# Latent attention in a two-layer decoder: two late weight splits and one late set of key copies placed between its first steps, and the low part of its values one step behind the rounding

## The chip, the core and the metric

The program runs on one core of one Trainium2 chip. The time is the device time of the whole program in microseconds, from one launch that computes all of the two layers. All arithmetic in question is in fp32 and in fp32r, a rounded form that TensorE takes; a number is held as a high part (rounded) and a low part (the difference), and a product is made of three matmuls: high by high, low by high, high by low.

## The reference, cut to what matters

The reference is a two-layer causal decoder on a (1, 512, 1024) input. Layer 0 runs a latent attention (8 heads) and a differential attention (4 heads) side by side, layer 1 two other attentions; each layer ends in a gated convolutional feed-forward. The part that the change touches is the latent attention of layer 0:

```python
c_q, c_kv, k_rope, dq, dk, dv = split_cols(h @ w_in, EVEN_SPLITS)
q = heads_first(rms_norm(c_q, cq_g) @ w_uq, MLA_HEADS)
q_nope, q_rope = q[..., :MLA_NOPE], rope(q[..., MLA_NOPE:], pos)
kv = heads_first(rms_norm(c_kv, ckv_g) @ w_ukv, MLA_HEADS)
k_nope, v_mla = kv[..., :MLA_NOPE], kv[..., MLA_NOPE:]
...
s = (jnp.einsum('bhqd,bhkd->bhqk', qn, k_nope)
     + jnp.einsum('bhqr,bkr->bhqk', qr, k_rope)).astype(jnp.float32) * scale
s = jnp.where(kpos[None, :] <= qpos[:, None], s, -jnp.inf)
p = jax.nn.softmax(s, axis=-1)
return jnp.einsum('bhqk,bhkd->bhqd', p.astype(v.dtype), v)
```

## The kernel before

The sequence of 512 tokens is cut into 4 tiles of 128. Activations stand transposed (features on the partitions), and every weight passes through one stream, the class `Weights`. A unit of the stream is a block of 128 x 1024. It is loaded into a raw buffer (three of them, `wraw`) on SyncE's queue, ScalarE rounds it into `wh` (L84, a CAST in the profile), and VectorE subtracts, `wl = wraw - wh` (L85). There are five pairs of `wh` and `wl`. `W.next()` hands out the next unit, having made `W.depth` units from there on; `W.ahead(n)` makes units up to number n. A raw buffer is loaded again only when VectorE has subtracted from it, so the place of a split also sets when the load of a later unit leaves SyncE's queue. The helper `mm3` (L325, L326, L327) issues the three matmuls of a product.

The latent attention lies between about 43 and 117 us of the span. It has two stages.

**Projections** (L1120 to L1157 of the program before). Six blocks `auq` make the queries: VectorE multiplies four of them by a table of the rotary angles (L1138, tiles `mq`, sixteen instructions in all), ScalarE scales the other two (L1135). Four products `auk` make the keys of two heads each, which ScalarE copies into `mk` (L1151, L1152), and four products `auv` make the values, which it copies into `mv` (L1157). The TensorE order here is written by hand; ScalarE's and VectorE's are the scheduler's.

**Steps** (L1161 to L1259). A unit of work is a pair of heads `p2` and a tile `i` of 128 queries, 16 in all, with i running fastest. A unit of tile i has i+1 tiles of keys. Its parts are:

- `score`: TensorE multiplies queries by keys into two PSUM banks of the tag `s`, one for each head (`sps`, L1166). VectorE adds the mask and finds the minimum (L1170; the profile calls it CUSTOM_DVE_ANT_0), which frees the bank. ScalarE takes the exponential with its row sum (L1173).
- `shares`: VectorE's reciprocal (L1179) and two scalings (L1181).
- `turn`: TensorE transposes the two matrices into the banks `t` and `n` (`tpp`, L1193); VectorE copies out the one (L1204), ScalarE the other (L1202).
- `value`, once for each pair of heads: TensorE multiplies the transposed shares by `mv` into the bank `o` (L1211); what it returns is the split of that bank into the high part `omh` (ScalarE, L230) and the low part `oml` (VectorE, L231).

There are only two `s` banks, so the scores of one unit need the mask step of the unit before to be done. Between the parts stand `fill`s, pieces of another projection that TensorE can do at any time: the values `av` of the differential attention, 32 pieces of three matmuls, in the order of the weight blocks. Its weights are four units of the stream, `wv[0]` to `wv[3]`, each used for two pieces of a query tile.

The list `plan` (18 rows) orders it. In row n come: `score(n)`; one entry of `left`, if there is one; some fills; `value`, if unit n-2 was the last of its heads; `turn(n-1)`; `shares(n)`; some fills. At n = 8, and at the end, one and two further units of the stream are split. TensorE, VectorE and ScalarE issue in exactly the order written there. After it comes the differential attention, whose first scores (`sps<-dqk`, L1311) the scheduler may place between the last rows of the plan.

Each engine issues its own list strictly in that order, so an instruction that waits holds all behind it on the same engine.

Of the kernel before, what the change touches and what calls it, by code (L numbers as in the profile page):

```python
# [9 lines left out]
F32 = mybir.dt.float32  # L10
# [3 lines left out]
ALU = mybir.AluOpType  # L14
# [84 lines left out]
def trunk(tc, A, out):  # L99
    nc = tc.nc  # L100
    PE, ACT, DVE, POOL = nc.tensor, nc.scalar, nc.vector, nc.gpsimd

    with ExitStack() as top:
# [15 lines left out]
        def bank(tag, name, *shape):  # L119

            t = pp.tile([P, S], F32, tag=tag, name=name, bufs=BANKS[tag])
            if not shape:
                return t[:]
            n = math.prod(shape)
            names = "abc"[:len(shape)]
            return t[:, :n].rearrange(f"p ({' '.join(names)}) -> p {' '.join(names)}",
                                      **dict(zip(names, shape)))
# [78 lines left out]
        units = []  # L206
# [15 lines left out]
        W = Weights(nc, wpool, units, 5)  # L222
# [6 lines left out]
        def split(h, l, src):  # L229
            ACT.copy(h, src)  # L230
            DVE.tensor_tensor(l, src, h.bitcast(F32), ALU.subtract)  # L231
# [632 lines left out]
        def even():  # L864
            with ExitStack() as es:
# [3 lines left out]
                def new_qk():  # L869
# [5 lines left out]
                oM = (ap.tile([P, 4, S], F32R, tag="omh", name="omh"),  # L875
                      ap.tile([P, 4, S], F32R, tag="oml", name="oml"))
# [12 lines left out]
                raw = dv[:, 0:2].rearrange("p a b -> p (a b)")  # L889
# [19 lines left out]
                with ExitStack() as e1:  # L909
# [3 lines left out]
                    mv = mp.tile([P, NT, 512], F32, tag="mv", name="mv")  # L913
# [143 lines left out]
                    def diff_qk(h, z):  # L1057
                        acc = bank("a", "aqk")
                        wh, wl = W.next()
                        for k in range(KD):  # L1060
                            mm3(acc, wh[:, k * P:(k + 1) * P], wl[:, k * P:(k + 1) * P],
                                xh[:, k], xl[:, k], k == 0, k == KD - 1)
                        put_qk(h, z, acc)
                        round_qk()
                        split_qk()

                    with e2:
# [50 lines left out]
                        for z in range(2):  # L1118
                            diff_qk(0, z)
                        ch, cl = cT  # L1120
                        uq = [W.next() for _ in range(2)]
                        kvh, kvl = W.next()

                        def q_block(n):

                            acc = bank("a", "auq")
                            c = slice(n * P, (n + 1) * P)
                            for k in range(2):
                                mm3(acc[:], uq[k][0][:, c], uq[k][1][:, c], ch[:, k], cl[:, k], k == 0, k == 1)
                            lo, hi = slice(64, 96), slice(96, 128)  # L1130
                            h = n // 3 * 4 + n % 3
                            steps = [] if n % 3 > 1 else [(mq[h][0:96, :], slice(0, 96), 0), (mq[h][hi, :], lo, 1),
                                                          (mq[h + 2][lo, :], hi, 1), (mq[h + 2][hi, :], hi, 0)]
                            for z in () if steps else range(2):
                                ACT.activation(mq[h + z][0:64, :], acc[z * 64:(z + 1) * 64, :], AF.Copy,  # L1135
                                               scale=-(96 ** -0.5))
                            for o, r, z in steps:
                                DVE.tensor_tensor(o, acc[r], qtab[r, z], ALU.mult)  # L1138

                        with tc.manual_schedule(engines={PE.engine}):  # L1140
                            for p2, blocks in enumerate(((0, 1), (2, ), (3, 4), (5, ))):
                                for n in blocks:
                                    q_block(n)
                                he, ho = mk[2 * p2], mk[2 * p2 + 1]
                                for x in (he, ho):
                                    if x is not mk[0]:
                                        DVE.tensor_copy(x[64:128, :], mk[0][64:128, :])
                                acc = bank("tn"[p2 % 2], "auk")
                                mm3(acc[:], kvh[:, p2 * P:(p2 + 1) * P], kvl[:, p2 * P:(p2 + 1) * P],
                                    ch[:, 2], cl[:, 2], True, True)  # L1150
                                ACT.copy(he[0:64, :], acc[0:64, :])  # L1151
                                ACT.copy(ho[0:64, :], acc[64:128, :])  # L1152
                                i = p2
                                t = slice(i * P, (i + 1) * P)
                                acc = bank("ssoo"[p2], "auv")
                                mm3(acc[:], ch[:, 2, t], cl[:, 2, t], kvh[:, 512:], kvl[:, 512:], True, True)
                                ACT.copy(mv[:, i], acc[:])  # L1157

                    sc = e1.enter_context(tc.tile_pool(name="esc", bufs=1, reuse_waits="tile"))

                    def score(p2, i):  # L1161
                        w = (i + 1) * P
                        ps = [bank("s", "sps")[:, :w] for _ in range(2)]
                        for z in range(2):
                            h = 2 * p2 + z
                            PE.matmul(ps[z], mq[h][:, i * P:(i + 1) * P], mk[h][:, :w], start=True, stop=True)  # L1166
                        st = sc.tile([P, 8], F32, tag="st", name="st", bufs=3)
                        s = [sc.tile([P, S], F32, tag="s", name="s", bufs=4)[:, :w] for _ in range(2)]
                        for z in range(2):
                            DVE.tensor_tensor_reduce(out=s[z], in0=ps[z], in1=mmask[:, 384 - i * P:S], scale=1.0,  # L1170
                                                     scalar=3e38, op0=ALU.add, op1=ALU.min, accum_out=st[:, z:z + 1])
                        for z in range(2):
                            ACT.activation(s[z], s[z], AF.Exp, bias=st[:, z:z + 1], scale=-1.0,  # L1173
                                           accum_out=st[:, 2 + z:3 + z])
                        return s, st
# [30 lines left out]
                    def value(p2):  # L1206
                        o = bank("o", "o")
                        for j in range(NT):
                            for y in range(2):
                                h = 2 * p2 + y  # L1210
                                PE.matmul(o[y * 64:(y + 1) * 64, j * P:], mv[:, j, h * 64:(h + 1) * 64],  # L1211
                                          pts[p2, y][:, off[j]:off[j + 1]], start=(j == 0), stop=(j == NT - 1))
                        return lambda: split(oM[0][:, p2], oM[1][:, p2], o)

                    def diff_v(i):
                        t = slice(i * P, (i + 1) * P)
# [10 lines left out]
                            ACT.activation(dv[:, i], a, AF.Copy, scale=r_tok[:, i:i + 1])  # L1227
                        yield

                    depth, W.depth = W.depth, 0  # L1230
                    wv = [W.next() for _ in range(4)]
                    fills = [f for i in range(NT) for f in [diff_v(i)] * KD]
                    units = [(p2, i) for p2 in range(4) for i in range(NT)]
                    plan = [(3, 0), (1, 0), (1, 0), (2, 0)] + [(3, 0), (0, 1), (1, 0), (2, 0)] * 3 + [(2, 2), (0, 0)]
                    scored, left = {}, []

                    def fill(n):
                        for _ in range(n):
                            next(fills.pop(0))

                    with tc.manual_schedule(engines={PE.engine, DVE.engine, ACT.engine}):
                        for n, (before, behind) in enumerate(plan):
                            if n < len(units):
                                scored[n] = score(*units[n])
                            if left:
                                left.pop(0)()
                            fill(before)
                            if n >= 2 and units[n - 2][1] == NT - 1:
                                left.append(value(units[n - 2][0]))
                            if n and n <= len(units):  # L1250
                                turn(*units[n - 1], scored.pop(n - 1)[0])
                            if n < len(units):
                                shares(scored[n])
                            fill(behind)
                            if n == 8:
                                W.ahead(W.pos + 1)
                        left.pop(0)()
                        W.ahead(W.pos + 2)
                    W.depth = depth  # L1259

# [162 lines left out]
                units = [(h, i) for h in range(4) for i in (3, 2, 0, 1)]  # L1423
# [631 lines left out]
```

## Time and profile before

| | |
|---|---|
| time, median of 3 runs | 1100.66 us (1100.39 to 1101.49) |
| the profiled execution's own time | 1100.6 us |
| its span | 1098.8 us |
| TensorE busy with matmuls, share of the span | 99% |
| TensorE's weight loads, share of the span | 87% |
| VectorE, ScalarE, GpSimd busy | 83%, 59%, 12% |
| mean granted TensorE clock | 0.999 |

The profile names engines PE (TensorE's matmuls), PEld (its weight loads), DVE (VectorE), ACT (ScalarE), POOL (GpSimd) and SP (SyncE). A row of the timeline has the start in us from the span's start, the time until the end of the last instruction of the row, the engine, the line, the operation, `out<-in`, the shapes, the number of instructions, and in brackets the idle time of the engine before the row and what ended it. A matmul's end is modelled and matmuls overlap, so TensorE's rows are read here by their starts: the time from one start to the next is what a row occupies of TensorE's list.

### The profile page before, as it was taken

Reading aid. Unit: us, or ns where it says so; the run is one execution under the profiler, and the core shown is the slowest. Engines: PE = TensorE matmul, PEld = TensorE weight load, DVE = VectorE, ACT = ScalarE, POOL = GpSimd, SP = SyncE. Lnnn points to the kernel's source line nnn. Section 1 sums busy time; section 2 is a strip of 40 time slices with the busy share of each in tenths; the row PEclk is TensorE's granted clock in tenths of the full one; section 3 lists DMA queues with packets and bytes.
Section 4 is the critical chain, followed back from the end, with each engine's and each line's share of the span. In section 5 each row is a group of like instructions: output and inputs, shape, how many; then the busy total and the mean of one; then the engine's idle time right before and its main releaser. Section 6 shows DMA issues by size and latency. Waiting matters only on the chain.

```text
span 1098.8 us, 18059 instructions
## 1 busy us (share of the span) xinstructions
PE 1089.2 (99%) x6724; PEld 954.7 (87%) x6724; DVE 907.2 (83%) x1528; ACT 648.6 (59%) x1108; POOL 126.7 (12%) x246
## 2 busy tenths in 40 slices
PE   9999999999999999999999999999999999999997
PEld 8866788898999999888888877889999999988886
DVE  6876786598999999998974775468989999999896
ACT  6555676346666765657553654555556666656562
POOL 3211133130000000000032111113100000000002
PEclk9999999999999999999999999999999999999999
DMA  7897998367566565345617999968846565535452
GB/s 266 268 237 211 247 293 230 106 199 208 161 185 192 174 187 168 125 163 175 234 53 269 276 289 296 276 182 234 224 141 192 174 190 176 192 123 174 147 198 78
DMA packets 72601, 217.26 MB, mean 198 GB/s; under 512 B 10048, under 2 KB 11200, under 8 KB 64320
## 3 DMA queue, kind: packets, MB, share of 16 engines
q1 hardware_dynamic: 61872, 147.73, 40.3%
q0 software_dynamic: 9920, 67.12, 24.3%
q10 hardware_dynamic: 720, 1.25, 0.4%
q8 instruction: 53, 0.87, 0.3%
q14 instruction: 36, 0.29, 0.1%
HBM read 208.69 MB, written 73.43 MB: 257 GB/s over the span
## 4 chain that ended last, share of the span: by engine, by line
PE 95%; DVE 3%; ACT 1%; issue 0%; DMA 0%; POOL 0%; POOLq 0%; DVEq 0%; SPq 0%; ACTq 0%
PE u L327 12%; PE u L325 12%; PE u L326 12%; PE acc L326 6%; PE acc L325 6%; PE acc L327 6%; PE apt L325 3%; PE apt L326 3%; PE apt L327 3%; PE ao L325 2%; PE ao L327 2%; PE ao L326 2%; PE aqk L325 1%; PE p L327 1%; PE p L326 1%; PE p L325 1%
## 5 line engine op out<-in xcount | busy, mean ns | idle before, releaser
L85 DVE TENSOR_TENSOR wl<-wraw,wh 128x1024 fp32r<-128x1024 f32 x246 | 298.0, 1217 | 38.2 <-ACT wh L84 37.8
L84 ACT CAST wh<-wraw 128x1024 fp32r<-128x1024 f32 x246 | 253.7, 1045 | 96.7 <-PE u L326 22.6
L327 PE MATMUL u<-xh,wl 128*128 128x256 f32 (+1 forms) x640 | 195.0, 305 | 0.0
L325 PE MATMUL u<-xh,wh 128*128 128x256 f32 (+1 forms) x640 | 195.0, 305 | 0.0
L326 PE MATMUL u<-xl,wh 128*128 128x256 f32 (+1 forms) x640 | 194.8, 304 | 0.0
L327 PEld LDWEIGHTS u<-xh,wl 128*128 128x128 f32 x640 | 122.2, 191 | 5.6 <-DVE wl L85 0.7
L326 PEld LDWEIGHTS u<-xl,wh 128*128 128x128 f32 x640 | 122.2, 191 | 5.0
L325 PEld LDWEIGHTS u<-xh,wh 128*128 128x128 f32 x640 | 122.2, 191 | 4.9
L325 PE MATMUL u<-gh,wh 128*128 128x256 f32 x384 | 108.7, 283 | 0.0
L327 PE MATMUL u<-gh,wl 128*128 128x256 f32 x384 | 108.7, 283 | 0.0
L326 PE MATMUL u<-gl,wh 128*128 128x256 f32 x384 | 108.6, 283 | 0.0
L326 PE MATMUL acc<-wl,gh 128*128 128x512 f32 (+1 forms) x234 | 90.8, 388 | 0.0
L327 PE MATMUL acc<-wh,gl 128*128 128x512 f32 (+1 forms) x234 | 90.6, 387 | 0.0
L325 PE MATMUL acc<-wh,gh 128*128 128x512 f32 (+1 forms) x234 | 90.2, 388 | 0.0
L238 POOL TENSOR_TENSOR rv<-ms,epst 128x1 f32<-128x1 f32 x31 | 12.3, 397 | 629.5 <-ACT junk L292 291.3
L489 ACT ACTIVATE y<-u,cw 128x512 f32<-128x512 f32 x88 | 67.7, 778 | 25.0 <-PE u L327 24.9
L326 PEld LDWEIGHTS u<-gl,wh 128*128 128x128 f32 x384 | 73.7, 192 | 0.1
L325 PEld LDWEIGHTS u<-gh,wh 128*128 128x128 f32 x384 | 73.7, 192 | 0.1
L327 PEld LDWEIGHTS u<-gh,wl 128*128 128x128 f32 x384 | 73.7, 192 | 0.0
L164 POOL DMA_DIRECT2D ws<-in_ffn_up_q x72 | 51.7, 726 | 153.6 <-DMA ws<-ws 74.5
L495 DVE SCALAR_TENSOR_TENSOR y<-u,cw,y 128x510 f32<-128x510 f32 x88 | 65.6, 747 | 2.2
L493 DVE SCALAR_TENSOR_TENSOR y<-u,cw,y 128x511 f32<-128x511 f32 x88 | 65.1, 743 | 2.0 <-ACT y L489 2.0
(391 smaller groups left out, 2473.5 us busy)
## 6 DMA issues: line engine op xcount, KB each, us to landing
ws<-in_ffn_up_q POOLq DMA_DIRECT2D x48, 768.0 KB, 13.3
wraw<-ws SPq DMA_DIRECT2D x128, 256.0 KB, 2.9
wraw<-in_ffn_up_q SPq DMA_DIRECT2D x96, 256.0 KB, 3.0
wraw<-in_ffn_w_down SPq DMA_DIRECT2D x44, 512.0 KB, 3.4
ws<-ws POOLq DMA_DIRECT2D x16, 768.0 KB, 13.1
ws<-in_ffn_up_q POOLq DMA_DIRECT2D x24, 512.0 KB, 6.5
wraw<-in_ffn_w_up SPq DMA_DIRECT2D x24, 512.0 KB, 4.7
wraw<-in_od_w_dqk SPq DMA_DIRECT2D x12, 512.0 KB, 9.8
```

Source lines behind the costliest of these rows:

```text
L84: self.nc.scalar.copy(h[:, :w], raw[:, :w])
L85: self.nc.vector.tensor_tensor(l[:, :w], raw[:, :w], h[:, :w].bitcast(F32), ALU.subtract)
L164: nc.gpsimd.dma_start(tiles[j][c][:].rearrange(wide, q=4), src.rearrange(wide, q=4), accum_op=op, max_dma_last_dim=8192)
L238: POOL.tensor_tensor(v[:, :n], ms, eps[:, :n], ALU.add)
L325: PE.matmul(o, lh, rh, start=first, stop=False, skip_group_check=more)
L326: PE.matmul(o, lh, rl, start=False, stop=False, skip_group_check=more)
L327: PE.matmul(o, ll, rh, start=False, stop=last, skip_group_check=more)
L489: ACT.activation(y[:, z], u[z], AF.Identity, bias=c[:, 3:4], scale=c[:, 2:3])
L493: DVE.scalar_tensor_tensor(y[:, z, 1:], u[z][:, :S - 1], c[:, 1:2], y[:, z, 1:], ALU.mult, ALU.add)
L495: DVE.scalar_tensor_tensor(y[:, z, 2:], u[z][:, :S - 2], c[:, 0:1], y[:, z, 2:], ALU.mult, ALU.add)
```

## The change

The change leaves every operation and its operands as they are and moves six groups of instructions.

- The look-ahead of the weight stream is lowered from 5 to 3 already at the start of the projections, so that only `wv[0]` and `wv[1]` are split there. The splits of `wv[2]` and `wv[3]` are issued in rows 0 and 1 of the plan: the rounding on ScalarE ahead of the row's `score`, the subtraction on VectorE behind it.
- The two key copies of the last pair of heads stand in row 0, behind its `score`, and the copy of the last tile of values in row 1, instead of behind their matmuls.
- Of the split of a `value`, the rounding takes one row's place in `left` and the subtraction the next row's.

```diff
@@ projections
                         ch, cl = cT
+                        depth, W.depth = W.depth, 3
                         uq = [W.next() for _ in range(2)]
...
-                                ACT.copy(he[0:64, :], acc[0:64, :])
-                                ACT.copy(ho[0:64, :], acc[64:128, :])
+                                if p2 < 3:
+                                    ACT.copy(he[0:64, :], acc[0:64, :])
+                                    ACT.copy(ho[0:64, :], acc[64:128, :])
+                                mk_acc = acc
...
-                                ACT.copy(mv[:, i], acc[:])
+                                if p2 < 3:
+                                    ACT.copy(mv[:, i], acc[:])
...
+                    def copies(he=he, ho=ho, acc=mk_acc):
+                        ACT.copy(he[0:64, :], acc[0:64, :])
+                        ACT.copy(ho[0:64, :], acc[64:128, :])
@@ value
-                        return lambda: split(oM[0][:, p2], oM[1][:, p2], o)
+                        h, l = oM[0][:, p2], oM[1][:, p2]
+                        return [lambda: ACT.copy(h, o),
+                                lambda: DVE.tensor_tensor(l, o, h.bitcast(F32), ALU.subtract)]
@@ steps
-                    depth, W.depth = W.depth, 0
-                    wv = [W.next() for _ in range(4)]
+                    W.depth = 0
+                    wv = [W.next() for _ in range(2)]
+                    low, split_whole = [], W.split
+
+                    def split_high(h, l, raw, w):
+                        ACT.copy(h[:, :w], raw[:, :w])
+                        low.append(lambda: DVE.tensor_tensor(l[:, :w], raw[:, :w], h[:, :w].bitcast(F32), ALU.subtract))
...
                         for n, (before, behind) in enumerate(plan):
+                            if n < 2:
+                                W.split = split_high
+                                W.ahead(W.pos + 1)
+                                wv.append(W.next())
+                                W.split = split_whole
                             if n < len(units):
                                 scored[n] = score(*units[n])
+                            if n < 2:
+                                low.pop(0)()
+                            if n == 0:
+                                copies()
+                            if n == 1:
+                                ACT.copy(mv[:, 3], acc[:])
                             if left:
                                 left.pop(0)()
                             fill(before)
                             if n >= 2 and units[n - 2][1] == NT - 1:
-                                left.append(value(units[n - 2][0]))
+                                left.extend(value(units[n - 2][0]))
...
-                        left.pop(0)()
+                        while left:
+                            left.pop(0)()
```

How the lists of the engines change is shown at three places. The line numbers are those of the program that a list belongs to; L1170 and L1178, for instance, are the same mask step, L1138 and L1139 the same multiplication, L85 and L1246 the same subtraction.

VectorE at the start of the steps, before. The first rows are the last multiplications of the projections; `wl` are the subtractions of `wv[2]` and `wv[3]`:

```order
L1138 TENSOR_TENSOR mq_124<-auq,qtab 32x512
L85 TENSOR_TENSOR wl<-wraw,wh 128x1024 x2
L1138 TENSOR_TENSOR mq_124<-auq,qtab 32x512
L1170 ISA s,st<-sps,mmask 128x128
L1170 ISA st 128x1
L1170 ISA s,st<-sps,mmask 128x128
L1170 ISA st 128x1
L1179 RECIPROCAL st<-st 128x2
L1181 TENSOR_SCALAR s<-s,st 128x128 x2
L1170 ISA s,st<-sps,mmask 128x256
```

The same place in the changed program:

```order
L1139 TENSOR_TENSOR mq_124<-auq,qtab 32x512 x2
L1178 ISA s,st<-sps,mmask 128x128
L1178 ISA st 128x1
L1178 ISA s,st<-sps,mmask 128x128
L1178 ISA st 128x1
L1246 TENSOR_TENSOR wl<-wraw,wh 128x1024
L1187 RECIPROCAL st<-st 128x2
L1189 TENSOR_SCALAR s<-s,st 128x128 x2
L1178 ISA s,st<-sps,mmask 128x256
L1178 ISA st 128x1
L1178 ISA s,st<-sps,mmask 128x256
L1246 TENSOR_TENSOR wl<-wraw,wh 128x1024
```

The mask step of unit 0 now stands ahead of both subtractions, and one of them behind each of the first two mask steps.

ScalarE there, before (`mk` are the late key copies, `mv` the copy of the last values):

```order
L84 CAST wh<-wraw 128x1024 x2
L1135 ACTIVATE mq_123<-auq 64x512
L1135 ACTIVATE mq_124<-auq 64x512
L1151 COPY mk_131<-auk 64x512
L1152 COPY mk_132<-auk 64x512
L1157 COPY mv<-auv 128x512
L1173 ACTIVATE s,st<-s,st 128x128 x2
L1173 ACTIVATE s,st<-s,st 128x256 x2
```

And in the changed program:

```order
L1245 CAST wh<-wraw 128x1024
L1136 ACTIVATE mq_123<-auq 64x512
L1136 ACTIVATE mq_124<-auq 64x512
L1181 ACTIVATE s,st<-s,st 128x128 x2
L1166 COPY mk_131<-auk 64x512
L1167 COPY mk_132<-auk 64x512
L1245 CAST wh<-wraw 128x1024
L1181 ACTIVATE s,st<-s,st 128x256 x2
L1271 COPY mv<-auv 128x512
```

The exponentials of unit 0 passed the two key copies, the value copy and the second rounding, and the rounding of `wv[3]` now stands behind the key copies.

VectorE around a low part, before (units 6 and 7; the second and third pair of heads read alike):

```order
L1170 ISA s,st<-sps,mmask 128x384
L1170 ISA st 128x1
L231 TENSOR_TENSOR oml<-o,omh 128x512
L1204 COPY pt<-tpp 128x2x128
L1179 RECIPROCAL st<-st 128x2
L1181 TENSOR_SCALAR s<-s,st 128x384 x2
L1170 ISA s,st<-sps,mmask 128x512
```

And in the changed program:

```order
L1212 COPY pt<-tpp 128x2x128
L1187 RECIPROCAL st<-st 128x2
L1189 TENSOR_SCALAR s<-s,st 128x384 x2
L1178 ISA s,st<-sps,mmask 128x512
L1178 ISA st 128x1
L1178 ISA s,st<-sps,mmask 128x512
L1178 ISA st 128x1
L1223 TENSOR_TENSOR oml<-o,omh 128x512
L1212 COPY pt<-tpp 128x2x128
```

The subtraction moved from ahead of the copy, the shares and the next unit's mask step to behind that mask step. This happens for three of the four pairs of heads; the last pair's stays where it was.

TensorE at the end of the steps, before (`sps<-dqk` are the first scores of the differential attention, `tpp` the transposes of unit 15):

```order
L326 MATMUL av<-wl,xh 128x512
L327 MATMUL av<-wh,xl 128x512
L1311 MATMUL sps<-dqk_92 128x512 x2
L1193 MATMUL tpp<-ident,s 128x128 x8
L325 MATMUL av<-wh,xh 128x512
```

And in the changed program, the last transposes and the last `value`:

```order
L327 MATMUL av<-wh,xl 128x512
L1201 MATMUL tpp<-ident,s 128x128 x8
L325 MATMUL av<-wh,xh 128x512
L326 MATMUL av<-wl,xh 128x512
L327 MATMUL av<-wh,xl 128x512
...
L1219 MATMUL o<-pt,mv 64x128 x2
L1339 MATMUL sps<-dqk_92 128x512 x2
```

The first two scores of the differential attention went from ahead of unit 15's transposes to behind the last `value`. The lists of GpSimd and SyncE are the same as before.

## The prediction

> **What bounds the kernel now.** I read the page first, then the chain of waits, then the timeline of each engine between 45 and 118 us, where the change lies.
>
> ```profile
> span 1098.8 us, 18059 instructions
> PE 1089.2 (99%) x6724; PEld 954.7 (87%) x6724; DVE 907.2 (83%) x1528; ACT 648.6 (59%) x1108; POOL 126.7 (12%) x246
> PE 95%; DVE 3%; ACT 1%; issue 0%; DMA 0%; POOL 0%; POOLq 0%; DVEq 0%; SPq 0%; ACTq 0%
> ```
>
> TensorE carries 95% of the chain that ends last. In order of time, the chain's last two pieces off TensorE are these; between them it is TensorE alone:
>
> ```profile
> 111.56 0.50 DVE s L1181
> ...
> 1083.87 0.70 DVE uu L777
> ```
>
> So whatever TensorE's list gains up to 112 us reaches the end of the program nearly whole, since no DMA and no other engine has a piece of the chain for the 970 us after it. The question is how much TensorE stands still between 56 and 118 us. The rows of its timeline, by their starts:
>
> ```profile
> 58.26 0.39 PE L326 MATMUL av<-wl,xh 128*128 128x512 f32 x1
> 58.49 0.39 PE L327 MATMUL av<-wh,xl 128*128 128x512 f32 x1
> 59.54 1.13 PE L1166 MATMUL sps<-mk,mq 128*128 128x256 f32 x4 [0.66 <-DVE st L1170]
> ...
> 64.04 1.91 PE L1166 MATMUL sps<-mk,mq 128*128 128x512 f32 x4
> ...
> 67.16 0.82 PE L1193 MATMUL tpp<-ident,s 128*128 128x128 f32 x6
> 67.81 0.61 PE L1166 MATMUL sps<-mk,mq 128*128 128x128 f32 x4
> 68.18 0.47 PE L325 MATMUL av<-wh,xh 128*128 128x512 f32 x1
> ...
> 80.97 0.82 PE L1193 MATMUL tpp<-ident,s 128*128 128x128 f32 x6
> 81.63 0.78 PE L1166 MATMUL sps<-mk,mq 128*128 128x128 f32 x4
> 82.16 0.48 PE L325 MATMUL av<-wh,xh 128*128 128x512 f32 x1
> ...
> 94.93 0.84 PE L1193 MATMUL tpp<-ident,s 128*128 128x128 f32 x6
> 95.77 1.10 PE L1166 MATMUL sps<-mk,mq 128*128 128x128 f32 x4
> 96.62 0.48 PE L325 MATMUL av<-wh,xh 128*128 128x512 f32 x1
> ...
> 111.55 0.49 PE L1311 MATMUL sps<-dqk 64*128 64x512 f32 x2
> 112.19 1.06 PE L1193 MATMUL tpp<-ident,s 128*128 128x128 f32 x8
> ...
> 116.89 0.73 PE L1311 MATMUL sps<-dqk,dqk 64*128 64x512 f32 x4
> 117.45 0.28 PE L1311 MATMUL sps<-dqk 64*128 64x256 f32 x2
> ```
>
> Only one row has idle time in brackets, but the starts tell of four places:
>
> - Start: a matmul of 512 columns takes 0.23 (58.26 to 58.49), yet from 58.49 to the scores of unit 1 it is 1.05. Lost: 0.82.
> - The transposes and scores around units 4, 8 and 12 are the same work. At unit 4 they take 0.65 and 0.37 (67.16, 67.81, 68.18), at unit 8 0.66 and 0.53. Lost: 0.17.
> - At unit 12, 0.84 and 0.85. Lost: 0.67.
> - The first two scores of the differential attention hold TensorE for 0.64 (111.55 to 112.19). Four of them at 116.89 take 0.56, so two are worth 0.28. Lost: 0.36, while the next transposes wait for the shares that the chain names at 111.56.
>
> Together 2.02 us. [...] The busy rows alone would allow a gain of 0.66 (the one bracket), so 1100.6 - 0.66 = 1099.9; the starts allow 2.02. [...]
>
> **The change, part by part.** Why TensorE waits at 59.54, and what VectorE and ScalarE do there:
>
> ```profile
> 45.42 10.62 DVE L1138 TENSOR_TENSOR mq<-auq,qtab 96x512 f32<-96x512 f32 x15
> 56.07 2.36 DVE L85 TENSOR_TENSOR wl<-wraw,wh 128x1024 fp32r<-128x1024 f32 x2
> 58.46 0.70 DVE L1138 TENSOR_TENSOR mq<-auq,qtab 32x512 f32<-32x512 f32 x1
> 59.19 0.29 DVE L1170 CUSTOM_DVE_ANT_0 s<-sps,mmask 128x128 f32<-128x128 f32 x1
> ...
> 61.72 0.29 DVE L1204 COPY pt<-tpp 128x128 f32<-128x128 f32 x1
> ...
> 62.61 0.17 DVE L1179 RECIPROCAL st<-st 128x2 f32<-128x2 f32 x1 [0.61 <-ACT s L1173]
> ...
> 63.35 0.55 DVE L1170 CUSTOM_DVE_ANT_0 s<-sps,mmask 128x384 f32<-128x384 f32 x1
> ```
>
> ```profile
> 54.70 2.00 ACT L84 CAST wh<-wraw 128x1024 fp32r<-128x1024 f32 x2
> 56.59 1.20 ACT L1135 ACTIVATE mq<-auq 64x512 f32<-64x512 f32 x2
> 57.80 0.58 ACT L1151 COPY mk<-auk 64x512 f32<-64x512 f32 x1
> ...
> 59.52 0.40 ACT L1173 ACTIVATE s<-s,st 128x128 f32<-128x128 f32 x1
> ```
>
> *Late splits on VectorE.* Fifteen multiplications end at 56.04; then two subtractions (1.18 each) hold the sixteenth and the mask step of unit 0 until 59.19. With them gone from there, the sixteenth runs 56.04 to 56.74, and unit 0's mask step, two heads of about 0.25, is done at 57.3. TensorE comes to unit 1's scores at 58.49 + 0.23 = 58.72 and finds the banks free: 0.82 gained, with 1.4 to spare.
>
> The 2.36 now stand further back, and what matters is unit 2's mask step, since TensorE's scores of unit 3 wait for it. The first subtraction fits between the mask steps of units 0 and 1. The second waits for its rounding. ScalarE: rounding of `wv[2]` 54.70 to 55.7, two scalings to 56.9, unit 0's two exponentials (0.40 each) 57.1 to 57.9, two key copies (0.58 each) to 59.1, rounding of `wv[3]` to 60.1. So the second subtraction runs 60.1 to 61.3. Behind it stand the same copy, reciprocal and scalings that took 61.72 to 63.35 before, 1.63 with 0.61 of idle in it, thus 1.0: unit 2's mask step starts at 62.3 and frees its first bank 0.6 later, at 62.9. TensorE wants it when unit 3's scores come up: 4.50 after unit 1's (59.54 to 64.04), so at 58.72 + 4.50 = 63.2. There is 0.3 of cover. If that is gone (say unit 1's exponentials, queued behind the second rounding, hold the reciprocal), the cost is what the idle of 0.61 hid, less the cover: at most 0.3. I take 0, nearest to the rows as they add up, and keep 0.3 for the range.
>
> The fills need `wl` of `wv[2]` only in row 2 and `wv[3]` in row 3, after 60.5; both are made by 61.3, and the first piece with `wv[3]` comes behind unit 3's scores.
>
> *Key and value copies.* The 1.16 + 0.59 of copies now stand behind unit 0's exponentials. The keys are those of heads 6 and 7, wanted 35 us later at unit 12; the values are wanted by the first `value` at about 72 us. The key product's bank is `n`, which unit 0's second transpose wants at about 60.5; the copies end at 59.1. Cost 0, with 1.4 of cover.
>
> *SyncE's queue.* Its list is the same, but a load leaves only when VectorE has emptied its buffer: the loads behind `wv[2]` and `wv[3]` leave about 1 and 3 us later. The first unit so loaded is wanted at the plan's end near 117 us. Cost 0. GpSimd's list has nothing to do with these buffers.
>
> *The low part one step behind.* The rows around units 7, 10 and 11:
>
> ```profile
> 82.90 0.17 DVE L1179 RECIPROCAL st<-st 128x2 f32<-128x2 f32 x1 [0.50 <-ACT s L1173]
> ...
> 93.22 0.69 DVE L231 TENSOR_TENSOR oml<-o,omh 128x512 fp32r<-128x512 f32 x1 [1.43 <-ACT omh L230]
> ...
> 95.02 0.68 DVE L1170 CUSTOM_DVE_ANT_0 s<-sps,mmask 128x512 f32<-128x512 f32 x1
> ```
>
> VectorE waits 1.43 for the rounding, which stands behind unit 10's exponentials on ScalarE, and works 0.6 on it; only then come the shares of unit 10 and the mask step of unit 11 at 95.02, whose second head ends near 96.3, which is what TensorE's scores of unit 12 wait for. With the subtraction behind that mask step, the shares wait for the exponentials alone, and the rounding's 0.5 and the subtraction's 0.6 leave the way: unit 11's mask step starts about 1.1 earlier. That is more than the 0.67 lost at unit 12 and the 0.17 at unit 8, so both go. What the moved subtraction now holds up are unit 6's copies and unit 7's shares. But the reciprocal waited 0.50 for the exponentials there (row at 82.90), so 0.5 of its 0.6 is hidden, and the rest has TensorE's nine fills as cover, 9 x 0.23 = 2.1. Cost 0. TensorE itself comes 0.8 earlier from the start on, and all these engines with it, since their rows hang on TensorE's scores.
>
> *The end.* Unit 15's shares gain the same 1.1 less 0.1, and the two scores of the differential attention stand elsewhere: 0.64 goes at 111.55, 0.28 comes back behind the last `value`. Gain 0.36.
>
> *Sum.* 0.82 + 0.17 + 0.67 + 0.36 = 2.02, no cost taken: 1100.6 - 2.0 = 1098.6, for the profiled execution, which stands 0.06 under the median of 1100.66. Small waits around 61.5, between unit 0's transposes and unit 2's scores, I leave out; they would go too, worth 0.1 to 0.3, so I lean to 1098.5.
>
> [...] A moved subtraction meets an issue of GpSimd.
>
> ```profile
> 57.19 0.55 POOL L164 DMA_DIRECT2D ws<-ws  x1 [3.65 <-DMA ws<-in_ffn_up_q]
> ```
>
> Before, the second of two subtractions ran beside this issue, and the two took 2.36, 1.18 each: no lengthening shows. Were one blocked for the issue, the late subtraction would cost 0.55, of which 0.3 is covered: 1098.8. [...] I give it a chance of 0.05, within the small-gain rival below.
>
> **Rivals.**
>
> *The early gain holds, the later ones do not.* The low part returns one step later, on the same VectorE, and at unit 12 another thing is late: a further weight split stands at n = 8, just ahead of units 9 to 11. Then the gain is 0.82 alone, or 0.5 with a cost of 0.3 at unit 3: 1099.8 to 1100.1. For it speaks that TensorE has little idle time in the busy rows. Against it speaks the 1.43 at 93.22, which no other work fills. Chance 0.20.
>
> *Slower.* ScalarE becomes the wait in the first units. It now has two roundings, two key copies and a value copy among the exponentials, 1.0 + 1.16 + 0.59 = 2.75 behind the first, and VectorE's second subtraction, 1.18, behind the rounding. If the exponentials of units 1 and 2 come late by all of that and the fills do not cover it, 2.75 + 1.18 = 3.9 is exposed at units 1 to 3, and a late chain also undoes the 1.2 of the later gains: 1100.6 - 0.8 + 3.9 = 1103.7. It decides if unit 2's mask step starts later than 62.6 on the old scale. Against it: by the sums above it starts at 62.3 with idle time to spare. Chance 0.05.
>
> That the change would not do what it says is not open: the lists show every move.
>
> **How the numbers follow.** The forecast, that all four places go, has 0.75 and its own range 1098.0 to 1099.0: 2.02, less 0.4, or plus the small waits and some of the 0.3 that I left out. A change of 0.2% is 2.2 us, about what a measurement of this kernel can tell from none, and lies inside: 1098.46. Of the 0.75 I put 0.42 under it and 0.33 above. So faster 0.42; same 0.33 + 0.20 = 0.53; slower 0.05. The range 1097.8 to 1100.0 leaves out the slower case, the low end of the small-gain rival, and gains over 2.9.
>
> **What would show it.** Right: no idle time ahead of unit 1's scores, and a step of 0.23 there; unit 12's transposes and scores at about 0.65 and 0.37; VectorE's wait for `omh` gone; the last `value` some 2.3 us earlier than before. Wrong in the start: a step over 0.5 ahead of unit 3's scores, or the reciprocal of unit 1 waiting on ScalarE. Wrong in the later part: the mask step of unit 11 still ending after TensorE asks for its bank. If the stage ends 2 us earlier but the span does not, the claim that the rest is TensorE alone was wrong.

## The result, and the profile after

| | before | the change |
|---|---|---|
| time, median of 11 runs each | 1100.81 us (1100.39 to 1101.85) | 1098.57 us (1097.9 to 1098.91) |
| ratio | | 0.9977, 95% interval 0.9969 to 0.9985 |
| the profiled execution's own time | 1100.6 us | 1098.23 us |
| its span | 1098.8 us | 1096.4 us |

The change is faster by 2.2 us by the medians, 0.23% by the ratio (0.15% to 0.31%). The forecast was 1098.5. The page of the changed kernel, its span, the busy times and the shares of the chain:

```profile
span 1096.4 us, 18060 instructions
PE 1088.1 (99%) x6724; PEld 956.0 (87%) x6724; DVE 907.4 (83%) x1528; ACT 648.9 (59%) x1108; POOL 127.4 (12%) x246
PE 98%; DVE 1%; issue 0%; ACT 0%; POOL 0%; POOLq 0%; DVEq 0%; ACTq 0%
```

The busy times are those of before to within about a microsecond. What changed is the chain: VectorE went from 3% to 1%, TensorE from 95% to 98%. Between 55 and 116 us the chain has no piece off TensorE any more.

TensorE's timeline after, at the places that the prediction read by their starts:

```profile
56.81 0.60 PE L1174 MATMUL sps<-mk,mq 128*128 128x128 f32 x4
...
59.08 0.39 PE L327 MATMUL av<-wh,xl 128*128 128x512 f32 x1
59.31 1.02 PE L1174 MATMUL sps<-mk,mq 128*128 128x256 f32 x4
...
63.06 0.60 PE L1201 MATMUL tpp<-ident,s 128*128 128x128 f32 x4
63.50 1.93 PE L1174 MATMUL sps<-mk,mq 128*128 128x512 f32 x4
64.86 0.79 PE L325 MATMUL av<-wh,xh 128*128 128x512 f32 x1
...
80.44 0.82 PE L1201 MATMUL tpp<-ident,s 128*128 128x128 f32 x6
81.10 0.61 PE L1174 MATMUL sps<-mk,mq 128*128 128x128 f32 x4
81.47 0.47 PE L325 MATMUL av<-wh,xh 128*128 128x512 f32 x1
...
94.26 0.82 PE L1201 MATMUL tpp<-ident,s 128*128 128x128 f32 x6
94.91 0.61 PE L1174 MATMUL sps<-mk,mq 128*128 128x128 f32 x4
95.28 0.47 PE L325 MATMUL av<-wh,xh 128*128 128x512 f32 x1
...
114.79 0.50 PE L1339 MATMUL sps<-dqk 64*128 64x512 f32 x2
115.13 0.64 PE L1339 MATMUL sps<-dqk,dqk 64*128 64x512 f32 x4
115.61 0.28 PE L1339 MATMUL sps<-dqk 64*128 64x256 f32 x2
...
116.05 0.50 PE L325 MATMUL aqk<-xh,wh 128*128 128x512 f32 x1
```

The step ahead of unit 1's scores is 0.23 (59.08 to 59.31), with no bracket. The transposes and scores around units 8 and 12 take 0.66 and 0.37, 0.65 and 0.37, as those around unit 4 did before. The first scores of the differential attention stand behind the last `value`, where the six of 512 columns take 0.82 in place of the 0.56 of four.

In the rest of this text "the stage" is the time from the start of unit 0's scores to the first `aqk` matmul of the differential attention. Before, those were 56.22 and 117.91, 61.69 us; after, 56.81 and 116.05, 59.24 us. The stage gained 2.45 us, the span 2.4.

### The profile page after: what moved, and what is told of

It is laid out like the page before. It is cut to its first block, busy times and chain, and to the rows that moved or that the text cites. A ratio compares the mean times of both kernels' runs of the same rounds, so it can differ in the third digit from the quotient of the medians.

```text
span 1096.4 us, 18060 instructions
## 1 busy us (share of the span) xinstructions
PE 1088.1 (99%) x6724; PEld 956.0 (87%) x6724; DVE 907.4 (83%) x1528; ACT 648.9 (59%) x1108; POOL 127.4 (12%) x246
## 4 chain that ended last, share of the span: by engine, by line
PE 98%; DVE 1%; issue 0%; ACT 0%; POOL 0%; POOLq 0%; DVEq 0%; ACTq 0%
PE u L327 12%; PE u L325 12%; PE u L326 12%; PE acc L326 6%; PE acc L325 6%; PE acc L327 6%; PE apt L325 3%; PE apt L326 3%; PE apt L327 3%; PE ao L325 2%; PE ao L327 2%; PE ao L326 2%; PE sps L1174 2%; PE aqk L325 1%; PE p L327 1%; PE p L325 1%
## 5 line engine op out<-in xcount | busy, mean ns | idle before, releaser
L85 DVE TENSOR_TENSOR wl<-wraw,wh 128x1024 fp32r<-128x1024 f32 x244 | 295.3, 1217 | 36.8 <-ACT wh L84 36.3
```

Of the source, the lines that this page charges most:

```text
L85: self.nc.vector.tensor_tensor(l[:, :w], raw[:, :w], h[:, :w].bitcast(F32), ALU.subtract)
```

## The experiments

All were profiled; those with an interval were also timed beside the kernel before. The stage is read off the starts of TensorE's rows, and in this stage two profiles of the same kernel agree to 0.03 us (61.69 and 61.72 for the kernel before), so it tells much smaller things apart than the time. Each ratio is to runs of before made beside the kernel, whose medians were 1100.96 (e1, e2), 1101.32 (e5) and 1100.73 us (e7).

| kernel | stage, us | against the change | time, us | ratio to before |
|---|---|---|---|---|
| before | 61.69 | +2.45 | 1100.81 | |
| the change | 59.24 | | 1098.57 | 0.9977 (0.9969 to 0.9985) |
| e1, the start alone | 60.61 | +1.37 | 1099.65 | 0.9990 (0.9981 to 0.9999) |
| e2, the low part alone | 60.35 | +1.11 | 1099.84 | 0.9988 (0.9979 to 0.9997) |
| e3, splits back | 60.55 | +1.31 | 1100.03, one run | |
| e4, copies back | 59.81 | +0.57 | 1098.79, one run | |
| e5, second subtraction twice | 60.54 | +1.30 | 1099.82 | 0.9986 (0.9977 to 0.9996) |
| e6, second rounding twice | 60.34 | +1.10 | 1100.93, one run | |
| e7, second subtraction a row later | 59.20 | -0.04 | 1098.64 | 0.9980 (0.9970 to 0.9990) |
| e8, the same, twice | 60.22 | +0.98 | 1100.34, one run | |
| e9, before again | 61.72 | +2.48 | 1101.36, one run | |

**e1, the start alone.** The low part is put back beside its rounding.

```diff
-                        h, l = oM[0][:, p2], oM[1][:, p2]
-                        return [lambda: ACT.copy(h, o),
-                                lambda: DVE.tensor_tensor(l, o, h.bitcast(F32), ALU.subtract)]
+                        return [lambda: split(oM[0][:, p2], oM[1][:, p2], o)]
```

> The start alone: the late splits and late copies as in the change, the low part of the values back beside its rounding. Theory A (each wait of TensorE has its own cause): the step ahead of unit 1's scores is 0.23 as in the change, the small waits at units 1 and 2 are gone, but unit 8 still loses 0.1 to 0.2, unit 12 about 0.6 and the two early scores of the differential attention about 0.35. The stage ends 0.9 to 1.1 us earlier than before, the time is about 1.0 us under that of before. Theory B (the start alone makes the gain, since all later steps then come earlier): units 8 and 12 lose nothing and the time is 2.0 to 2.4 us under that of before.

Theory A held: the stage is 1.08 us shorter than before. TensorE around unit 12, and VectorE ahead of it:

```profile
94.40 0.85 PE L1201 MATMUL tpp<-ident,s 128*128 128x128 f32 x6
95.25 1.10 PE L1174 MATMUL sps<-mk,mq 128*128 128x128 f32 x4
96.11 0.47 PE L325 MATMUL av<-wh,xh 128*128 128x512 f32 x1
```

```profile
92.70 0.69 DVE L231 TENSOR_TENSOR oml<-o,omh 128x512 fp32r<-128x512 f32 x1 [1.42 <-ACT omh L230]
...
94.50 0.68 DVE L1178 CUSTOM_DVE_ANT_0 s<-sps,mmask 128x512 f32<-128x512 f32 x1
```

The 0.85 and 0.86 and VectorE's wait of 1.42 for the rounding are those of before within 0.01, although everything comes a microsecond earlier, counted from unit 0's scores: VectorE's list hangs on TensorE's scores, and an earlier start moves both alike.

**e2, the low part alone.** The kernel before, with only the two lines of `value` changed and `left` extended by two entries.

> The low part alone: the subtraction of a value one step behind its rounding, the splits and copies of the start as before. Theory A: the step ahead of unit 1's scores stays at 1.05, units 8 and 12 lose nothing, the scores of the differential attention stand behind the last value; the time is 1.1 to 1.4 us under that of before. Theory B: unit 12 still waits, the gain is under 0.4 us.

Theory A held: the stage is 1.34 us shorter than before. The start is that of before:

```profile
59.07 0.39 PE L327 MATMUL av<-wh,xl 128*128 128x512 f32 x1
60.12 1.13 PE L1166 MATMUL sps<-mk,mq 128*128 128x256 f32 x4 [0.66 <-DVE st L1170]
```

Units 8 and 12 lose nothing, and the early scores of the differential attention went behind the last `value`. That last move comes from the low part: with it alone they moved, with the start alone they stayed. The two halves add up: 1.08 + 1.34 = 2.42, against 2.45 for both.

**e3, splits back.** The change, with the look-ahead of 5 left until the steps, four units of `wv` taken ahead of them, and none split in rows 0 and 1; copies and low part as in the change.

> The change with its two weight splits back ahead of the steps, and the key and value copies left late. Theory A (VectorE's two subtractions are what TensorE waited for): as with the low part alone, the step ahead of unit 1's scores is 1.05 again, within 0.1, and the stage gains 1.1 to 1.4 us. Theory C (the copies on ScalarE were in the way of unit 0's exponentials and held the start): the step falls below 0.6.

The step ahead of unit 1's scores was 1.05 again and the stage gained 1.14, so theory A held and C fell: the subtractions, not the copies, held the start.

```profile
59.03 0.39 PE L327 MATMUL av<-wh,xl 128*128 128x512 f32 x1
60.08 1.13 PE L1173 MATMUL sps<-mk,mq 128*128 128x256 f32 x4 [0.66 <-DVE st L1177]
```

But the late copies cost 0.2 here that e2 does not pay:

```profile
61.74 0.27 PE L1200 MATMUL tpp<-ident,s 128*128 128x128 f32 x1
62.19 0.33 PE L1200 MATMUL tpp<-ident,s 128*128 128x128 f32 x1 [0.18 <-ACT mk L1166]
```

Unit 0's second transpose waits for the key copy, which holds bank `n`. Behind unit 0's exponentials the copies are free only if those exponentials are early, and that needs the splits out of the way.

**e4, copies back.** The change, with the key and value copies in their old place.

```diff
-                                if p2 < 3:
-                                    ACT.copy(he[0:64, :], acc[0:64, :])
-                                    ACT.copy(ho[0:64, :], acc[64:128, :])
+                                ACT.copy(he[0:64, :], acc[0:64, :])
+                                ACT.copy(ho[0:64, :], acc[64:128, :])
```

> The change with the key and value copies back in their old place, ahead of unit 0's exponentials. Theory A: unit 1's scores still come without a wait; but unit 0's exponentials start about 1.5 us later, behind 1.75 us of copies, VectorE's reciprocal waits for them about 1 us, and the mask step of unit 2 comes about 0.5 later, so TensorE loses 0.4 to 0.7 ahead of the scores of units 2 and 3 together. Theory D (the copies are hidden wherever they stand): the stage is as long as in the change, within 0.1.

The stage is 0.57 longer than in the change; theory A held. VectorE behind the first late subtraction:

```profile
57.62 1.22 DVE L1244 TENSOR_TENSOR wl<-wraw,wh 128x1024 fp32r<-128x1024 f32 x1
59.86 0.17 DVE L1185 RECIPROCAL st<-st 128x2 f32<-128x2 f32 x1 [1.02 <-ACT s L1179]
```

In the change the reciprocal follows the subtraction with no wait:

```profile
57.80 1.22 DVE L1246 TENSOR_TENSOR wl<-wraw,wh 128x1024 fp32r<-128x1024 f32 x1
58.93 0.16 DVE L1187 RECIPROCAL st<-st 128x2 f32<-128x2 f32 x1
```

In e4 it waits 1.02 for exponentials that stand behind 1.75 us of copies.

**e5, the second subtraction twice.** How much cover is there?

```diff
-                                low.pop(0)()
+                                low[0]()
+                                if n == 1:
+                                    low[0]()
+                                low.pop(0)
```

> The change with the subtraction of its second late split done twice, the same values written again: 1.15 us more on VectorE between the mask steps of units 1 and 2. Theory A as predicted (0.3 of cover ahead of unit 3's scores): TensorE loses 0.8 to 0.9 there. Theory E (there is no cover at all, as the step of 0.48 in place of 0.46 ahead of unit 3's second matmul hints): it loses 1.0 to 1.2. Theory F (the fills of TensorE hide it): under 0.3. The rest of the program passes the loss on whole in A and E.

The stage grew by 1.30 us. VectorE's list, in e5 and then in the change, from the subtraction to the copy behind it:

```profile
60.74 2.48 DVE L1246 TENSOR_TENSOR wl<-wraw,wh 128x1024 fp32r<-128x1024 f32 x2
63.15 0.28 DVE L1212 COPY pt<-tpp 128x128 f32<-128x128 f32 x1
```

```profile
60.76 1.22 DVE L1246 TENSOR_TENSOR wl<-wraw,wh 128x1024 fp32r<-128x1024 f32 x1
61.91 0.28 DVE L1212 COPY pt<-tpp 128x128 f32<-128x128 f32 x1
```

Two subtractions hold the list for 2.41, one for 1.15, so the repeat added 1.26 and not the 1.15 that was expected, and TensorE lost all of it: no cover at all. Theory E is the nearest, and its range was short because the added work was taken too small; A and F fell. Where it is lost, in TensorE's timeline:

```profile
62.80 0.40 PE L327 MATMUL av<-wh,xl 128*128 128x512 f32 x1
63.94 0.76 PE L1201 MATMUL tpp<-ident,s 128*128 128x128 f32 x4 [0.75 <-DVE s L1189]
64.68 1.98 PE L1174 MATMUL sps<-mk,mq 128*128 128x512 f32 x4
```

First at unit 1's transposes (62.80 to 63.94, 0.91 over a step of 0.23), which wait for unit 1's shares, and only then at unit 3's scores (0.74 for transposes that take 0.44).

**e6, the second rounding twice.** The rounding of `wv[3]` on ScalarE is repeated in the same way.

> The change with the rounding of its second late split done twice, the same values written again: 0.95 us more on ScalarE, behind unit 0's exponentials and ahead of unit 1's. Theory E (no cover): the subtraction starts 0.95 later and TensorE loses 0.8 to 1.0 ahead of unit 3's scores. Theory A (0.3 of cover): 0.6 to 0.7. Theory G (the rounding is early enough that VectorE never waits for it): under 0.2.

The two roundings hold ScalarE's list for 2.03 (60.14 to 62.17) where one holds it for 0.94 (59.69 to 60.63 in the change), so 1.09 was added and not the 0.95 that was expected. The stage grew by 1.10 us, again by all of it; G fell, and E is nearest. The rounding and VectorE's second subtraction, which now waits for it:

```profile
60.14 2.12 ACT L1246 CAST wh<-wraw 128x1024 fp32r<-128x1024 f32 x2
62.17 0.51 ACT L1181 ACTIVATE s<-s,st 128x256 f32<-128x256 f32 x1
```

```profile
62.29 1.23 DVE L1247 TENSOR_TENSOR wl<-wraw,wh 128x1024 fp32r<-128x1024 f32 x1 [1.04 <-ACT wh L1246]
```

So the change runs with VectorE and ScalarE both just in time there. Its own rows: the rounding starts at 59.69 and takes 1.04, the mask step ahead of the subtraction ends at 60.8, and the subtraction starts at 60.76 (its row stands under e5).

```profile
59.69 1.04 ACT L1245 CAST wh<-wraw 128x1024 fp32r<-128x1024 f32 x1
```

Unit 2's mask step, which comes behind that subtraction:

```profile
62.83 0.55 DVE L1178 CUSTOM_DVE_ANT_0 s<-sps,mmask 128x384 f32<-128x384 f32 x1
```

**e7 and e8, the second subtraction a row later.** In e7 it stands behind unit 2's mask step (`if n in (0, 2)` in place of `if n < 2`), in e8 also twice.

> The change with its second late subtraction one row further back, behind the mask step of unit 2 in place of that of unit 1; its rounding stays where the change has it. Theory E (in the change the place ahead of unit 3's scores has no cover): the little that is lost there, a step of 0.48 for 0.43, goes, the stage is 0.0 to 0.1 us shorter than in the change and the time the same within what can be measured. Theory H (the subtraction is wanted by the fills of row 3, so it is late there): TensorE loses more than 0.2 in rows 3 and 4.

> The same with that subtraction done twice in its new place, the same values written again: 1.15 us more on VectorE behind the mask step of unit 2. It asks how much cover there is in that place, where there was none a row earlier (twice there cost 1.30 of the stage). Theory E with the rows as they add up: unit 2's shares come before 66.2 on the scale of the change and unit 2's transposes are wanted at 66.5, so at most 0.4 is lost. Theory I (VectorE is as tight in every row of the first pair of heads): 1.0 or more is lost again.

e7 met theory E, and H fell: unit 1's transposes and unit 3's scores take 0.43 and 1.32 in place of 0.44 and 1.36, the stage is 0.04 shorter, hardly more than two profiles of one kernel differ, and the time cannot be told from the change's. It is no better kernel. e8 was expected to lose at most 0.4 and lost 1.02 against e7: theory I held, mine fell. It is lost at units 2 and 4:

```profile
66.80 0.85 PE L1201 MATMUL tpp<-ident,s 128*128 128x128 f32 x6 [0.16 <-DVE s L1189]
67.64 1.10 PE L1174 MATMUL sps<-mk,mq 128*128 128x128 f32 x4
68.50 0.47 PE L325 MATMUL av<-wh,xh 128*128 128x512 f32 x1
```

I had asked only whether unit 2's shares are in time. Behind them stands unit 3's mask step, and unit 4's scores wait for that. The repeat added about 1.26 to VectorE's list here too (63.31 to 65.71, against 63.12 to 64.25 in e7), so most of it is lost in this row, as all of it was in the row before.

**e9, before again.** Against one profile of before, the rows ahead of the stage seemed half a microsecond slower in every changed kernel.

> The kernel before, profiled a second time. From the first matmul to unit 0's scores the profile of before took 55.16 us and those of the change and the other kernels 55.57 to 56.20, though nothing there was changed. If that is of the execution and not of the program, this one takes 55.5 or more as well, and the stage itself 61.6 to 61.8 again. If it belongs to the program, it takes 55.2.

From the first matmul to unit 0's scores it took 55.72, so the difference is of the execution. From the first `aqk` matmul to the last matmul of the program the profiles range from 973.40 (the change) to 974.66 (e8), with before at 973.96 and 974.13, and nothing was changed there. That is how far one span can be trusted for a single microsecond.

## Why the prediction was right, step by step

**That the rest passes the gain on.** Right. No chain piece off TensorE lies between 116 and 1081 us after, and the span gained 2.4 of the stage's 2.45. That the two agree to 0.05 is partly chance: in this pair of profiles the start was 0.6 slower and the rest 0.56 faster, and both differences are within what unchanged parts show.

**The start, 0.82.** Right in cause (e3) and size: the step went from 1.05 to 0.23. Left out of the sum, and named only as 0.1 to 0.3, were the small waits behind it: unit 1's scores from 0.78 to 0.67, unit 0's transposes from 0.31 to 0.21 and unit 2's scores from 1.10 to 1.00. That is 0.30. But the late splits do not bring the 0.82 alone. With the copies left early the step is 0.23 as well (58.90 to 59.13 in e4), yet the stage gains only 0.54 by the splits (60.35 in e2, 59.81 in e4), since more is lost right behind: unit 1's transposes take 0.74 (63.08 to 63.82) in place of 0.44.

**No cost taken, 0.3 of cover at unit 3.** The cost was right, within the 0.04 that e7 gains; the cover was wrong. Unit 2's mask step started 6.02 after unit 0's scores (62.83 less 56.81) and was expected at 62.3 on the old scale, 6.08 after. But TensorE came to unit 3's scores at 63.50, 6.69 after, not 6.98 as the 4.50 from unit 1 to unit 3 of before had it: those 4.50 held the small waits that the change also removes. So the cover of 0.3 was just those 0.3, and nothing is left (e5). I had counted as spare time what was a wait of the thing that I was about to speed up. I also named unit 3's scores as the first to be late, and e5 shows unit 1's transposes ahead of them.

**Copies at no cost.** Right as far as it went: in the change the copies wait for nobody, and unit 0's transposes (60.87) come without a wait after the key copies' end (59.78). But the prediction priced them alone, as an edit that costs nothing and brings nothing. Moving them brings 0.57 of the 2.45 once the splits are late, since with the splits late and the copies early, the exponentials are what VectorE waits for (e4).

**The low part, 0.17 and 0.67.** Right: 0.16 and 0.67 went, and only with this edit (e1, e2). VectorE's wait for `omh` is gone ahead of three of the four low parts; ahead of the last pair's, which did not move, it is 3.60 as before (3.59), and the chain has no piece there. The lead was under-estimated. Unit 11's mask step:

```profile
91.13 0.42 DVE L1212 COPY pt<-tpp 128x256 f32<-128x256 f32 x1 [0.26 <-PE tpp L1201]
91.83 0.17 DVE L1187 RECIPROCAL st<-st 128x2 f32<-128x2 f32 x1 [0.27 <-ACT s L1181]
92.03 0.75 DVE L1189 TENSOR_SCALAR s<-s,st 128x384 f32<-128x384 f32 x2
92.69 0.69 DVE L1178 CUSTOM_DVE_ANT_0 s<-sps,mmask 128x512 f32<-128x512 f32 x1
```

It starts 35.88 after unit 0's scores and started 38.80 after before (95.02 less 56.22), 2.9 earlier. About 1.1 of that is the start (e1), so the low part brought 1.8 (1.7 in e2, alone) where 1.1 was worked out. The copy, too, now runs while VectorE would have waited: of the 1.43 ahead of `oml`, 0.53 is left, ahead of the copy and the reciprocal. TensorE could use only 0.67 of this lead, so the sum did not suffer.

**The end, 0.36.** The 0.64 went and 0.26 came back (0.82 less 0.56), 0.38. The last matmul ahead of those scores also had a step of 0.33 (111.22 to 111.55 before) for 0.23, 0.1 more.

**SyncE's queue at no cost.** Right: between 55 and 116 us of the changed kernel no engine but GpSimd waits for a DMA (GpSimd 53.6 us in all).

**The sum.** 2.02 was forecast and 2.45 measured in the stage; 0.30 and 0.1 of the difference are the waits just named. The lean to 1098.5 took part of that in.

**Busy rows or starts.** The one bracket on TensorE's rows, 0.66, would have given 1099.9. The starts gave 2.02 and the stage shows 2.45. The busy time does not show the gain: matmuls are busy for 1089.2 us before and 1088.1 after, 99% of the span in both, and weight loads for 954.7 and 956.0, 87% in both. The starts do.

**The issue of GpSimd.** In the change the second late subtraction (60.76, 1.22 long) does run beside an issue of GpSimd:

```profile
60.88 0.53 POOL L164 DMA_DIRECT2D ws<-ws  x1 [2.88 <-DMA ws<-in_ffn_up_q]
```

It takes 1.22 beside that issue. In e6, where the issue (61.14 to 61.66) is over before the subtraction starts at 62.29, it takes 1.23. The eleven subtractions of `wv[2]` and `wv[3]` in the profiles of before, the change, e4, e5 and e6 all take 1.217 to 1.226. So no lengthening shows, and the 0.55 that the prediction set on a blocked subtraction is shown by no run.

**The rivals.** The small gain fell by e1 and e2: each half brings its own share. The slower case did not come, but e6 shows that its mechanism is real and near: of 1.09 us more on ScalarE at that place, TensorE pays all. The point from which it decides was not 0.3 away, as the prediction had it, but zero.

## What to carry to other kernels

When one engine is busy nearly all the time, look for its hidden waits by comparing the start-to-start time of equal groups of instructions in its timeline; a few of them, each with its own cause, may sum to more than all idle time that the rows show (here 2.02 us against 0.66). Where work is moved into a gap, work out the cover on the times after the change, not on those before: waits that the same change removes look like spare time. And price edits together where one clears the way that another needs: the late copies were worth 0.57 us with the late splits and cost 0.2 without them.

## What the runs showed of the hardware

TensorE's first microseconds differ between executions of the same kernel. The four transposes near 4.5 us, in the first profile of before and then in its second:

```profile
4.51 0.60 PE L943 MATMUL tp<-ident,X 128*128 128x128 f32 x4
4.95 1.06 PE L927 MATMUL warm<-dqk 128*128 128x128 f32 x8
```

```profile
4.63 1.06 PE L943 MATMUL tp<-ident,X 128*128 128x128 f32 x4
5.48 1.22 PE L927 MATMUL warm<-dqk 128*128 128x128 f32 x8
```

They take 0.44 from start to start of the groups in the one and 0.85 in the other. Of the changed kernels e7 has 0.44, e4 and e8 have 0.76 and 0.78, the change and the rest 0.85. The granted clock reads 1.00 between 4.0 and 6.6 us in both profiles of before and in those of the change, e1, e2 and e6, so it does not tell the 0.44 from the 0.85, and no run here shows what does. From the first `ac` matmul behind these rows (6.55 us in the one, 7.12 in the other) to unit 0's scores nine of the eleven profiles take 49.63 to 49.68; e7 takes 49.83 and e6 50.14. So the half microsecond ahead of the stage is in these first rows, except that e6 has another half further on, whose cause is open.
